# Copies by bank, one moved input sum and one moved product in a one-core hybrid decoder step

## The chip, the cores and the metric

The kernel runs on one core of a Trainium2 chip. The metric is the device time of one execution in microseconds (us), as the median over several runs; less is better. A core has TensorE for matrix products, VectorE and ScalarE for element-wise work on SBUF and PSUM, GpSimd for element-wise work on SBUF, and queues on which SyncE, ScalarE and GpSimd issue DMA transfers. Products are written to PSUM, which has eight banks.

## What the reference computes

One step of a decoder layer for 1024 prompt tokens and 64 sample tokens (8 sequences of 8 tokens), with a width of 1024. After a root-mean-square norm, one input projection feeds three branches: retention, multi-scale causal pooling, and sparse attention with a compressed, a selected and a window part. Each branch has a gate and a projection of its own; they are merged by sigmoid gates, projected once more, added to the input and normed. Cut to what the change touches:

```python
z = rms_norm(x, gain) @ w_in
(rq, rk, rv, rg, pu, pg, nq, ck, cv, sk, sv, wk, wv, nbg, ng, mg) = jnp.split(z, split_at, axis=-1)
blk = kv_cmp.reshape(n, nc, L_CMP, 2, NSA_KV_HEADS, dh) + pe_cmp   # compressed blocks of 32 tokens
cm = jnp.mean(blk, axis=2)
kc = jnp.einsum('ncgd,de->ncge', cm[:, :, 0], w_ck)
vc = jnp.einsum('ncgd,de->ncge', cm[:, :, 1], w_cv)
...
b_c = (jax.nn.silu(ng) * o_c) @ w_br_c
merged = gates[:, :, 0] * b_a + gates[:, :, 1] * b_b + gates[:, :, 2] * b_c
y = x + merged @ w_out
y_prompt = rms_norm(hp, final_gain)
```

## The kernel before

Every fp32 matrix is kept as two fp16 parts, high and low, so that one product is three fp16 products on TensorE (high by high, high by low, low by high). A weight is loaded in fp32 as `raw` and split by `wsplit`: ScalarE writes the high part, VectorE the low part. Two `raw` buffers take turns in the projection stage; four of the first eight loads go to parts of the query weights' tiles instead.

The tokens are nine tiles of 128 (the last holds the 64 sample tokens). `phase_kv` is the projection stage: `norm_first` norms the first tile, and TensorE writes it transposed into two PSUM banks, from which ScalarE copies the high part (L379) and VectorE subtracts to get the low part (L380), piece by piece. `kv_tile` projects keys and values, `q_tile` the queries, `cmp_means` the means of blocks of 32 tokens, `cmp_weights` loads the weights of the compressed branch (seven loads on SyncE and two small products, L490). After the last tile `cmp_prompt` makes the compressed keys (`kc`) and values (`vc`) for two groups: two products, then copies on ScalarE (L562, L568) and subtractions on VectorE (L563, L569).

`input_sums` makes eight units of sums and differences of quarters of the normed input for a later stage that multiplies by Strassen's scheme. A unit is four additions (L1221) and four subtractions (L1223) on VectorE, a copy to fp16 on ScalarE (L1224), a subtraction on VectorE (L1225) and a store to DRAM on SyncE's queue (L1226). The units are made between the tiles, one or two at a time, the last at n = 8.

The attention stage follows. `silu_c` first makes the sparse branch's gate (four weight columns of three segments; a segment is 24 products and a step on ScalarE and VectorE; a `yield` follows each eighth of it), then the heads' scores, probabilities and values are made, with the retention branch's gate and other gate products as filling. Scores are written to four rotating buffers with the tag "S"; probabilities are transposed by DMA into `pt`. Retention, pooling, sample attention and the merge stage come next.

`out_rows` is the output stage. It makes the last projection for 512 rows of either half by Strassen's scheme, as seven products per tile of 128 rows, 12 matmuls of 512 columns each (L1841). In a first round over four tiles it forms "11 by 11" and "12 by 21", which need no weight difference. `remainder` does the 64 rows that are left (L1881). A second round over the four tiles forms the other five. The four differences T1 to T4 of the output weights are made at the stage's start by VectorE (L1800) and split (L222, L223). `plus` adds a product to a row tile on VectorE (L1846).

The order in which each engine runs its instructions is fixed before the run by a planner that simulates the program with modelled times and gives priority to what is written first. `with self.behind()` puts each instruction of a block behind the last marked instruction on its own engine; `self.tc.issue_after(x)` does so only for the engine of x. Instructions that touch one PSUM bank on different engines are ordered one after the other.

Of the kernel before, what the change touches and what calls it, by code (L numbers as in the profile page):

```python
# [127 lines left out]
class Kern:  # L128
# [32 lines left out]
    def run(self):  # L161
        ctx = self.ctx
        right = ExitStack()
        self.setup(ctx)
        with ExitStack() as es:
            self.kvstore(es)
            with ExitStack() as e1:
                self.phase_kv(e1)
            rp = self.pool(right, "gate", side="right")
            self.ga = rp.tile([P, 8, NG, 2, 32], F16, tag="ga", name="ga", bufs=1)  # L170
            self.rp = rp
            self.gc = rp.tile([P, 4, NG, 2, 32], F16, tag="gc", name="gc", bufs=1)
            with ExitStack() as e1:
                sp = self.pool(e1, "attw", bufs=2)

                tp = self.pool(e1, "atth")
                ps = self.pool(e1, "aps", bufs=1, space=PSUM)
                self.pjb = A_PJ
                self.wq = self.nc.scalar
                self.eq = self.nc.scalar  # L180
                self.egd = self.dr.tile([8, P, NTOK], F32, name="egd")
                self.cgd = self.dr.tile([8, P, NTOK], F32, name="cgd")
                with self.behind():
                    deque(self.silu_c(tp, self.gc, C_NG, ps, self.wng), 0)
                fill = chain(self.silu_c(tp, self.ga, C_RG, ps), self.early_gates(tp, ps, range(N_FILL)))
                self.prompt_attention(sp, ps, fill)
                with self.tc.issue_after(self.after.ins):
                    deque(fill, 0)
                self.eq = self.nc.sync
        with ExitStack() as eo:  # L190
            self.smc = self.pool(eo, "smc")
            self.pjb = R_PJ
            with ExitStack() as es:
                self.psb, ppj, psa = [self.pool(es, x, bufs=1, space=PSUM) for x in ("rpsb", "rppj", "rpsa")]
                self.retention(es, ppj, psa, right)
            self.gbp = self.pool(right, "gbp", side="right")
            self.gb = self.gbp.tile([P, 4, NG, 2, 32], F16, tag="gb", name="gb", bufs=1)
            with ExitStack() as es:
                psb, ps, pst = [self.pool(es, x, bufs=1, space=PSUM) for x in ("spsb", "sppj", "spst")]
                sp = self.pool(es, "smp", bufs=1)  # L200
                pool = self.pooling(es, ps, pst)
                next(pool)
                with self.behind():
                    self.sample_attention(sp, psb, pst)
                next(pool, None)
                self.out_weights(self.pool(es, "wout"))
        with ExitStack() as es:
            self.output(es)
        right.close()
        if self.post:  # L210
            self.post(self)
# [143 lines left out]
    def norm_first(self, xp, ps):  # L355

        nc, d = self.nc, self.d
        x = self.load_x(xp, 0)
        nc.sync.dma_start(self.ident, d["c_ident"])
        gcol = xp.tile([P, 8], F32, name="gcol", bufs=1)  # L360
        nc.sync.dma_start(gcol, d["gain_cols"])
        xs = xp.tile([P, 1024], F32, tag="xs", name=self.nm("xs"), bufs=2)
        ss = xp.tile([P, 2], F32, tag="ss", name=self.nm("ss"), bufs=2)
        nc.scalar.activation(xs[:, :512], x[:, :512], AF.Square, accum_out=ss[:, 0:1])
        nc.vector.tensor_tensor_reduce(out=xs[:, 512:], in0=x[:, 512:], in1=x[:, 512:], scale=1.0, scalar=0.0,
                                       op0=ALU.mult, op1=ALU.add, accum_out=ss[:, 1:2])
        nc.vector.tensor_tensor(ss[:, 0:1], ss[:, 0:1], ss[:, 1:2], op=ALU.add)
        self.rsqrt(ss[:, 1:2], ss[:, 0:1], 1.0 / 1024)
        dg = xp.tile([P, P], F32, name="dg", bufs=1)
        nc.vector.tensor_scalar(dg, self.ident, ss[:, 1:2], None, op0=ALU.mult)  # L370
        self.first = []
        for q in range(2):
            tp = ps.tile([P, 4, P], F32, tag="tk", name=self.nm("tp"), bufs=2)
            for k in range(4):
                kk = q * 4 + k
                nc.tensor.matmul(tp[:, k, :], x[:, kk * P:(kk + 1) * P], dg, start=True, stop=True)
            for k in range(4):
                kk = q * 4 + k
                self.marks["ACT"] = nc.scalar.activation(self.xh[:, kk, :P], tp[:, k], AF.Copy, scale=gcol[:, kk:kk + 1])  # L379
                self.marks["DVE"] = nc.vector.scalar_tensor_tensor(  # L380
                    self.xl[:, kk, :P], tp[:, k], gcol[:, kk:kk + 1], self.xh[:, kk, :P],
                    op0=ALU.mult, op1=ALU.subtract)
            self.first.append(dict(self.marks))
# [117 lines left out]
    def phase_kv(self, es):  # L501
# [22 lines left out]
        for n in range(NT + 1):  # L524
            if n == 0:
                qh, ql = self.load_t(wk, [(C_NQ, 512)], "nq", 1, out=nq)
            if n + 2 < NT:
                self.norm_tile(kp, ps, gain, TILES[n + 2])
            if n == 0:
                self.cmp_weights(bp, ps)  # L530
            if n < NT:
                kvz = self.kv_tile(kp, bp, ps, kh, kl, TILES[n])
            if n:
                self.q_tile(kp, ps, qh, ql, TILES[n - 1])
            if n == NT:
                self.cmp_prompt(kp, ps, cmt)
            if n < NT and TILES[n] < 8:
                with self.tc.issue_after(self.marks["PE"].ins):
                    self.cmp_means(ps, kvz, cmt, TILES[n])
            if n == 3:  # L540
                self.bias_tables(bp, ps)

            if n == 4:
                sums = self.input_sums(kp)
            with self.behind():
                for _ in range((0, 0, 0, 0, 1, 2, 2, 2, 1, 0)[n]):
                    next(sums)
            if n == 7:
                with self.behind():
                    self.wng = self.load_c(d["w_in"][0][:, C_NG:C_NG + P])  # L550

    def cmp_prompt(self, kp, ps, cmt):
        nc = self.nc

        nc.vector.memset(self.vbd, 0.0)
        cmr = kp.tile([P, 4, 32], F32, name="cmr", bufs=1)
        nc.vector.tensor_copy(cmr, cmt[:, 1:2, :].to_broadcast([P, 4, 32]))
        for g in range(2):
            gr = slice(g * 64, g * 64 + 64)
            kc = ps.tile([P, 32], F32, tag="kc", name=self.nm("kc"), bufs=2)  # L560
            nc.tensor.matmul(kc, self.wckd[gr].rearrange("p a c -> p (a c)"), cmt[gr, 0, :], start=True, stop=True)
            nc.scalar.copy(self.kcst[:, g, 0, :], kc)  # L562
            nc.vector.tensor_tensor(self.kcst[:, g, 1, :], kc, self.kcst[:, g, 0, :], op=ALU.subtract)  # L563
            vc = ps.tile([P, 64], F32, tag="kc", name=self.nm("vc"), bufs=2)
            nc.tensor.matmul(vc, cmr[gr].rearrange("p a c -> p (a c)"), self.wcvd[gr], start=True, stop=True)
            for r in range(4):
                rr = slice(r * 32, r * 32 + 32)
                nc.scalar.copy(self.vbd[rr, g, 0, r, :], vc[rr])  # L568
                nc.vector.tensor_tensor(self.vbd[rr, g, 1, r, :], vc[rr], self.vbd[rr, g, 0, r, :], op=ALU.subtract)  # L569

    def kv_tile(self, kp, bp, ps, kh, kl, t):
# [635 lines left out]
                self.eq.dma_start(self.egd[e, :, s0:s0 + n], th[:, :n])  # L1207
                yield

    def input_sums(self, rp):  # L1210


        nc = self.nc
        self.txd = self.dr.tile([P, 4, 2, 4, 544], F16, name="txd")
        for c0 in (0, 272):
            for k in range(4):
                f = rp.tile([P, 4, 272], F32, tag="rsf", name=self.nm("rsf"), bufs=1)
                o = rp.tile([P, 4, 2, 272], F16, tag="rso", name=self.nm("rso"))
                for i, (kk, t) in enumerate(((k, 0), (k, 1), (k + 4, 1), (k + 4, 0))):
                    c = slice(t * 544 + c0, t * 544 + c0 + 272)  # L1220
                    nc.vector.tensor_tensor(f[:, i], self.xh[:, kk, c], self.xl[:, kk, c], op=ALU.add)  # L1221
# [1 line left out]
                    nc.vector.tensor_tensor(f[:, a], f[:, x], f[:, y], op=ALU.subtract)  # L1223
                nc.scalar.copy(o[:, :, 0], f)  # L1224
                nc.vector.tensor_tensor(o[:, :, 1], f, o[:, :, 0], op=ALU.subtract)  # L1225
                nc.sync.dma_start(self.txd[:, :, :, k, c0:c0 + 272], o)  # L1226
                yield

    def ga_at(self, j):
# [549 lines left out]
    def out_rows(self, ps, wk, mm, sx, wo, tb):  # L1779
# [116 lines left out]
        for i, c in enumerate(order):  # L1896
# [5 lines left out]
            nc.scalar.activation(u, p, AF.Copy, scale=IWS)  # L1902
            plus(x[:, :512], p, x[:, :512])
            plus(x[:, :512], prod("12", "21", c), x[:, :512])
            base.append((x, st, u))
        remainder()
        for i, c in enumerate(order):
# [7 lines left out]
            nc.gpsimd.tensor_tensor(b0, b0, u2, op=ALU.add)  # L1915
            p5 = prod("S1", "T1", c)
            plus(b0, p5, b0)
            plus(b0, prod("S4", "22", c), b0)
            square(x0, y0, s0, 1, P, 512, 512)
            finish(((0, c, P),), x0, y0, s0, P, 2)  # L1920
            plus(u3, prod("S3", "T3", c), u2)
# [46 lines left out]
```

## Time and profile before

| | |
|---|---|
| median of 3 runs | 1310.8 us (1307.58 to 1311.88) |
| the profiled execution's own time | 1306.29 us |
| its span, first to last instruction | 1304.5 us |
| mean granted TensorE clock | 0.987 |

The profile is of a single execution. Its span is the time between its first and last instruction; 1.8 us of its own time lie outside. All times of rows are counted from the start of the span.

### The profile page before, as it was taken

How to read it: one execution, taken by the hardware profiler on the slowest of the kernel's cores; microseconds unless marked ns; L12 is line 12 of the kernel's file. 1: busy time of each engine (PE TensorE's matmuls, PEld its weight loads, DVE VectorE, ACT ScalarE, POOL GpSimd, SP SyncE). 2: the span in 40 equal slices, each digit the busy share in tenths (PEclk: the TensorE clock that was granted, in tenths of full speed). 3: DMA queues.
4: the chain of work that ended last, by engine and by line, in shares of the span. 5: the costliest groups of instructions: out<-in, count | busy, mean ns of one | idle time of the engine just before them, and what ended most of it. 6: DMA issues, size and time to landing. Idle time of an engine off the chain costs nothing. (4 is left out here: it accounts for less than half of the span.)

```text
span 1304.5 us, 27795 instructions
## 1 busy us (share of the span) xinstructions
PE 1251.3 (96%) x10520; PEld 850.6 (65%) x10520; DVE 912.2 (70%) x2288; ACT 631.3 (48%) x1474; POOL 525.2 (40%) x561
## 2 busy tenths in 40 slices
PE   7999899989999989999999999999999999999997
PEld 4555566767677764555655565657788888888643
DVE  6648635788777864766766668663698877578975
ACT  5633436667676763555554454433544333213331
POOL 1122013567676751445553550101743566323133
PEclk9999899999999999999999999998999999999998
DMA  7766623698899996243741278327542211543632
GB/s 251 182 133 149 149 66 86 99 147 146 164 173 205 192 207 174 58 124 104 173 139 35 85 202 264 77 76 255 180 130 58 58 49 55 175 145 114 227 96 97
DMA packets 324315, 179.24 MB, mean 137 GB/s; under 512 B 204433, under 2 KB 298609, under 8 KB 323764
## 3 DMA queue, kind: packets, MB, share of 16 engines
q1 hardware_dynamic: 283844, 137.83, 45.3%
q10 hardware_dynamic: 35600, 26.32, 6.8%
q0 software_dynamic: 4736, 13.31, 3.2%
q8 instruction: 82, 1.34, 0.4%
q14 instruction: 53, 0.43, 0.1%
HBM read 98.80 MB, written 33.25 MB: 101 GB/s over the span
## 5 line engine op out<-in xcount | busy, mean ns | idle before, releaser
L761 POOL TENSOR_TENSOR hl<-S,hl 128x640 f16<-128x640 f32 (+7 forms) x128 | 153.8, 1210 | 142.5 <-DVE hl L760 96.6
L309 PE MATMUL pj<-xh,whi 128*128 128x384 f16 (+1 forms) x480 | 153.0, 319 | 2.4 <-ACT ue L1423 2.1
L310 PE MATMUL pj<-xl,whi 128*128 128x384 f16 (+1 forms) x480 | 153.0, 319 | 0.0
L311 PE MATMUL pj<-xh,wlo 128*128 128x384 f16 (+1 forms) x480 | 152.8, 318 | 0.0
L288 PE MATMUL z<-rwh,xh 128*128 128x512 f16 x256 | 97.0, 379 | 0.0
L290 PE MATMUL z<-rwh,xl 128*128 128x512 f16 x256 | 97.0, 379 | 0.0
L289 PE MATMUL z<-rwl,xh 128*128 128x512 f16 x256 | 97.0, 379 | 0.0
L756 ACT ACTIVATE S<-S,nm 128x640 f32<-128x640 f32 (+7 forms) x128 | 93.7, 732 | 5.2 <-DVE hst L852 0.9
L311 PEld LDWEIGHTS <-wlo 128*128 128x128 f16 x672 | 66.1, 98 | 36.6 <-issue 1.3
L310 PEld LDWEIGHTS <-whi 128*128 128x128 f16 x672 | 66.1, 98 | 36.1 <-issue 4.9
L1572 DVE TENSOR_TENSOR q<-st,q 128x288 f32<-128x288 f32 (+1 forms) x168 | 70.3, 433 | 26.4 <-PE st L1563 25.3
L309 PEld LDWEIGHTS <-whi 128*128 128x128 f16 x672 | 66.1, 98 | 33.6 <-issue 1.3
L288 PEld LDWEIGHTS <-xh 128*128 128x128 f16 x448 | 45.3, 101 | 46.4 <-issue 7.2
L290 PEld LDWEIGHTS <-xl 128*128 128x128 f16 x448 | 43.9, 98 | 44.9 <-issue 0.7
L222 ACT ACTIVATE whi<-raw 128x1024 f16<-128x1024 f32 (+1 forms) x48 | 45.5, 948 | 57.0 <-PE pj L310 14.7
L289 PEld LDWEIGHTS <-xh 128*128 128x128 f16 x448 | 43.9, 98 | 42.1 <-issue 0.9
L755 ACT ACTIVATE hl<-S,nm 128x128 f16<-128x128 f32 (+7 forms) x64 | 49.1, 767 | 36.6 <-DMA pt<-hl 36.5
L1328 PE MATMUL o<-vst,pt 128*128 128x64 f16 x528 | 56.3, 193 | 10.7 <-DMA pt<-hl 10.6
L760 DVE CAST hl<-S 128x640 f16<-128x640 f32 (+4 forms) x64 | 33.2, 519 | 45.9 <-ACT S L756 16.2
L1260 POOL TENSOR_TENSOR rh<-rot,rh 128x256 f16<-128x256 f32 (+1 forms) x36 | 26.5, 735 | 89.1 <-ACT rh L1259 88.9
L310 PE MATMUL eg<-xl,whi 128*128 128x384 f16 (+1 forms) x192 | 61.5, 320 | 0.0
L309 PE MATMUL eg<-xh,whi 128*128 128x384 f16 (+1 forms) x192 | 61.5, 320 | 0.0
(511 smaller groups left out, 4056.0 us busy)
## 6 DMA issues: line engine op xcount, KB each, us to landing
raw<-w_in SPq DMA_DIRECT2D x26, 512.0 KB
raw<-w_in ACTq DMA_DIRECT2D x18, 512.0 KB
raw<-w_in SPq DMA_DIRECT2D x48, 128.0 KB
wad<-q ACTq DMA_DIRECT2D x21, 256.0 KB
txd<-rso SPq DMA_DIRECT2D x8, 544.0 KB
raw<-egd SPq DMA_DIRECT2D x16, 272.0 KB
s<-state_ret SPq DMA_DIRECT2D x16, 256.0 KB
o_ret_s<-s POOLq DMA_DIRECT2D x16, 256.0 KB
```

Source lines behind the costliest of these rows:

```text
L222: a = nc.scalar.activation(hi, raw, AF.Copy, scale=WS)
L288: nc.tensor.matmul(out, xh, hi[:, k, c0:c0 + n], start=(k == 0), stop=False)
L289: nc.tensor.matmul(out, xh, lo[:, k, c0:c0 + n], start=False, stop=False)
L290: self.marks["PE"] = nc.tensor.matmul(out, xl, hi[:, k, c0:c0 + n], start=False, stop=(k == 7))
L309: nc.tensor.matmul(out, hi[:, k, :], xh, start=(k == 0), stop=False)
L310: nc.tensor.matmul(out, hi[:, k, :], xl, start=False, stop=False)
L311: self.filled = nc.tensor.matmul(out, lo[:, k, :], xh, start=False, stop=(k == 7))
L755: nc.scalar.activation(hl[:, :w], s[:, d0:c1], AF.Exp, bias=nm[:, br:br + 1], scale=0.125)
L756: nc.scalar.activation(s[:, c0:c1], s[:, c0:c1], AF.Exp, bias=nm[:, br:br + 1], scale=0.125, accum_out=l[:, 0, br, r:r + 1])
L761: nc.gpsimd.tensor_tensor(hl[:, w:2 * w], s[:, d0:c1], hl[:, :w], op=ALU.subtract)
L1328: nc.tensor.matmul(out, lhs[0], rhs[0], start=start, stop=False)
L1572: nc.vector.tensor_tensor(out[:, c0:c0 + n], b, x[:, c0:c0 + n], op=ALU.add)
```

## The change

Five edits. In the first tile, the four copies of a bank are written before its four subtractions. The compressed branch's weights are asked for behind the first tile's projection, with their products behind its last one. In `cmp_prompt` a group's keys and values share one bank, each group has a bank of its own, both products come first, and all copies precede the subtractions. The last unit of the input sums is made behind the sparse branch's gate in program order, in two buffers of the scores' tag, and stored through GpSimd's queue; the first gate segment is placed behind TensorE's mark alone. In the output stage, the product S4 by 22 moves from the second round to the first.

```diff
@@ run
+                score = lambda: sp.tile([P, 1664], F32, tag="S", name=self.nm("sum"), bufs=LAG + 1)
+                self.sums_room = lambda: (score()[:, :1088].rearrange("p (i c) -> p i c", i=4),
+                                          score()[:, :1088].bitcast(F16).rearrange("p (i a c) -> p i a c", i=4, a=2))
+                self.sums_queue = self.nc.gpsimd
+                gates = self.silu_c(tp, self.gc, C_NG, ps, self.wng)
+                with self.tc.issue_after(self.marks["PE"].ins):
+                    for _ in range(8):
+                        next(gates)
                 with self.behind():
-                    deque(self.silu_c(tp, self.gc, C_NG, ps, self.wng), 0)
+                    deque(gates, 0)
+                    deque(self.sums, 0)
@@ norm_first
                 self.marks["ACT"] = nc.scalar.activation(self.xh[:, kk, :P], tp[:, k], AF.Copy, scale=gcol[:, kk:kk + 1])
+            for k in range(4):
+                kk = q * 4 + k
                 self.marks["DVE"] = nc.vector.scalar_tensor_tensor(
@@ phase_kv
-            if n == 0:
-                self.cmp_weights(bp, ps)
             if n < NT:
                 kvz = self.kv_tile(kp, bp, ps, kh, kl, TILES[n])
+            if n == 0:
+                with self.tc.issue_after(self.marks["PE"].ins):
+                    self.cmp_weights(bp, ps)
...
-                sums = self.input_sums(kp)
+                self.sums_room = lambda: (kp.tile([P, 4, 272], F32, tag="rsf", name=self.nm("rsf"), bufs=1),
+                                          kp.tile([P, 4, 2, 272], F16, tag="rso", name=self.nm("rso")))
+                self.sums_queue = nc.sync
+                sums = self.sums = self.input_sums()
             with self.behind():
-                for _ in range((0, 0, 0, 0, 1, 2, 2, 2, 1, 0)[n]):
+                for _ in range((0, 0, 0, 0, 1, 2, 2, 2, 0, 0)[n]):
@@ cmp_prompt
-        for g in range(2):
+        for g, tag in enumerate(("kc", "cm")):
             gr = slice(g * 64, g * 64 + 64)
-            kc = ps.tile([P, 32], F32, tag="kc", name=self.nm("kc"), bufs=2)
+            cc = ps.tile([P, 96], F32, tag=tag, name=self.nm("kc"), bufs=1)
+            kc, vc = cc[:, :32], cc[:, 32:]
             nc.tensor.matmul(kc, self.wckd[gr].rearrange("p a c -> p (a c)"), cmt[gr, 0, :], start=True, stop=True)
+            nc.tensor.matmul(vc, cmr[gr].rearrange("p a c -> p (a c)"), self.wcvd[gr], start=True, stop=True)
+            rows = [slice(r * 32, r * 32 + 32) for r in range(4)]
             nc.scalar.copy(self.kcst[:, g, 0, :], kc)
+            for r, rr in enumerate(rows):
+                nc.scalar.copy(self.vbd[rr, g, 0, r, :], vc[rr])
             nc.vector.tensor_tensor(self.kcst[:, g, 1, :], kc, self.kcst[:, g, 0, :], op=ALU.subtract)
-            vc = ps.tile([P, 64], F32, tag="kc", name=self.nm("vc"), bufs=2)
-            nc.tensor.matmul(vc, cmr[gr].rearrange("p a c -> p (a c)"), self.wcvd[gr], start=True, stop=True)
-            for r in range(4):
-                rr = slice(r * 32, r * 32 + 32)
-                nc.scalar.copy(self.vbd[rr, g, 0, r, :], vc[rr])
+            for r, rr in enumerate(rows):
                 nc.vector.tensor_tensor(self.vbd[rr, g, 1, r, :], vc[rr], self.vbd[rr, g, 0, r, :], op=ALU.subtract)
@@ input_sums
-                f = rp.tile([P, 4, 272], F32, tag="rsf", name=self.nm("rsf"), bufs=1)
-                o = rp.tile([P, 4, 2, 272], F16, tag="rso", name=self.nm("rso"))
+                f, o = self.sums_room()
...
-                nc.sync.dma_start(self.txd[:, :, :, k, c0:c0 + 272], o)
+                self.sums_queue.dma_start(self.txd[:, :, :, k, c0:c0 + 272], o)
@@ out_rows, first round
             plus(x[:, :512], prod("12", "21", c), x[:, :512])
+            plus(x[:, 512:], prod("S4", "22", c), x[:, 512:])
@@ out_rows, second round
             plus(b0, p5, b0)
-            plus(b0, prod("S4", "22", c), b0)
             square(x0, y0, s0, 1, P, 512, 512)
```

## Rows read from the trace of the kernel before

**Rows 1.** The page: busy us, share of the span and instructions by engine.

```profile
PE 1251.3 (96%) x10520; PEld 850.6 (65%) x10520; DVE 912.2 (70%) x2288; ACT 631.3 (48%) x1474; POOL 525.2 (40%) x561
```

**Rows 2.** Busy time by stretch; last: granted clock, DMA share, GB/s.

```profile
7.00:17.00 10.00, 6.89 (x34) 4.90 (x33) 5.73 (x12) 5.99 (x14) 0.39 (x1) 1.00 0.97 345
17.00:21.00 4.00, 4.00 (x17) 2.62 (x17) 3.89 (x5) 3.66 (x7) 0.16 (x1) 0.57 0.59 179
138.00:147.00 9.00, 5.06 (x36) 3.16 (x33) 7.95 (x20) 6.05 (x14) 0.00 (x0) 0.82 0.60 137
147.00:151.00 4.00, 4.00 (x15) 1.91 (x15) 0.65 (x3) 1.40 (x4) 0.00 (x0) 0.54 1.22 290
151.00:191.00 40.00, 39.70 (x295) 25.81 (x294) 15.93 (x51) 15.69 (x46) 4.21 (x10) 1.00 0.36 84
1212.50:1233.30 20.80, 20.80 (x99) 9.36 (x96) 20.80 (x33) 9.89 (x18) 3.53 (x3) 1.00 0.73 246
1238.70:1243.00 4.30, 2.08 (x12) 0.80 (x9) 4.04 (x7) 3.78 (x9) 0.00 (x0) 0.99 0.55 184
1243.00:1247.00 4.00, 4.00 (x12) 1.47 (x11) 4.00 (x9) 3.12 (x8) 0.00 (x0) 0.58 0.00 0
```

**Rows 3.** TensorE's waits over the span: us in total, times, longest.

```profile
PE o L1328 <- DMA pt<-hl: 10.6, 12, 3.9
```

**Rows 4.** First tile: its copies, subtractions and their waits, then TensorE by time.

```profile
L379 ACT ACTIVATE xh<-tp,gcol x8: 358/367/368, 8.6 to 14.2; 128x128 f16<-128x128 f32 x8
  DVE xl L380: 2.5, 5
...
L380 DVE SCALAR_TENSOR_TENSOR xl<-tp,gcol,xh x8: 342/350/353, 9.0 to 14.6; 128x128 f16<-128x128 f32 x8
  ACT xh L379: 2.8, 6
...
15.36 0.49 PE L288 MATMUL pj<-kvh,xh 128*128 128x512 f16 x2 [1.37 <-ACT kvh L222]
16.50 0.57 PE L490 MATMUL pmps<-a,pe 32*128 32x1 f32 x4 [0.65 <-DMA pe<-pe_cmp]
```

**Rows 5.** The last key weight's load and splits by time, and the next hole.

```profile
17.57 0.38 SPq L255 DMA_DIRECT2D raw<-w_in  x1
20.73 0.86 ACT L222 ACTIVATE kvh<-raw 128x792 f16<-128x792 f32 x1 [0.34 <-DMA raw<-w_in]
23.48 0.98 DVE L223 SCALAR_TENSOR_TENSOR kvl<-raw,kvh 128x792 f16<-128x792 f32 x1
36.29 0.61 PE L612 MATMUL tk<-id,kd 128*128 128x128 f16 x8 [1.52 <-DVE xl L410]
```

**Rows 6.** Between projection and branch gates, by time.

```profile
140.13 1.50 DVE L1221 TENSOR_TENSOR rsf<-xh,xl 128x272 f32<-128x272 f16 x4
143.77 0.61 PE L695 MATMUL tq<-id,qs 64*64 64x64 f16 x8 [1.98 <-DVE qs L682]
146.50 0.69 PE L565 MATMUL vc<-wcvd,cmr 64*128 64x64 f32 x2 [1.56 <-DVE kcst L563]
```

**Rows 7.** The sums' lines: duration ns min/median/max, first and last start.

```profile
L1223 DVE TENSOR_TENSOR rsf<-rsf x32: 370/441/443, 84.8 to 145.5; 128x272 f32<-128x272 f32 x32
L1224 ACT CAST rso<-rsf x8: 1090/1096/1098, 86.9 to 150.2; 128x1088 f16<-128x1088 f32 x8
L1225 DVE TENSOR_TENSOR rso<-rsf,rso x8: 1291/1292/1539, 88.0 to 151.3; 128x1088 f16<-128x1088 f32 x8
```

**Rows 8.** Output stage by time, TensorE and VectorE.

```profile
1225.88 1.27 DVE L1846 SCALAR_TENSOR_TENSOR xr<-py,xr 128x512 f32<-128x512 f32 x2
1233.38 5.42 PE L1881 MATMUL py<-wo,mm 128*32 128x256 f16 x192
1242.81 0.93 PE L1841 MATMUL py<-tb,T 128*128 128x512 f16 x2 [1.91 <-DVE tb L223]
1247.67 0.69 DVE L223 SCALAR_TENSOR_TENSOR T4a<-q,T4a 128x512 f16<-128x512 f32 x1
```

More of the change, by code (lines that the diff above doesn't have):

```diff
@@ L1208, in early_gates, with input_sums @@
                 yield
-    def input_sums(self, rp):
+    def input_sums(self):
         nc = self.nc
```

## The prediction, made before the change was run

> **What bounds the kernel now.** I read the page first: TensorE is busy for 96% of the span, VectorE for 70% and no other engine for more than 48% [rows 1]. So time can only be won where TensorE stands still or runs at its lower clock, and the second view, the busy time by stretch, was used to find those places near the edits. There are three [rows 2]. In 7 to 17 us, where the first token tile is projected, TensorE is busy 6.89 of 10 us, and the next 4 us run at a granted clock of 0.57, that is mostly at 1.2 GHz. In 138 to 147 us, between the projection stage and the branch gates, it is busy 5.06 of 9 us, and the 4 us behind are granted 0.54. In 1238.7 to 1243 us, at the start of the output stage's second round, it is busy 2.08 of 4.30 us, and the 4 us behind are granted 0.58. The third view, TensorE's waits over the whole span, shows that the largest single cause lies elsewhere: 10.6 us in 12 holes for transposed probabilities [rows 3]. No edit is aimed at that. The last view, the order of instructions, tells which wait ends last in each of the three holes.
>
> What a hole costs is its idle time and the slow clock behind it. The slow part is worth, from the granted clock, (1 - 0.57) x 4 = 1.7 us at the start, (1 - 0.54) x 4 = 1.8 us at the stage change and (1 - 0.58) x 4 = 1.7 us in the output stage. The three ceilings are thus 3.11 + 1.7 = 4.8, 3.94 + 1.8 = 5.7 and 2.22 + 1.7 = 3.9 us, 14.4 us together.
>
> **Edit 1, the first tile's copies, and edit 2, the compressed keys' weights behind the tile.** Eight ScalarE copies of 0.37 us and eight VectorE subtractions of 0.35 us empty two banks. They alternate, copy and subtraction of one piece, and VectorE stood 2.8 us before six of its eight for a copy, ScalarE 2.5 us before five of its own [rows 4]. Nothing is added or removed; with four copies and then four subtractions a bank is handed over once, not seven times. I count one hand-over of the six waits per bank as left, 2 x 2.8/6 = 0.9 us, so VectorE's stream is 1.9 us shorter. The price is that the first subtraction comes three copies later, 3 x 0.37 = 1.1 us; TensorE has the copies' own products to do meanwhile, and if they don't cover it, it comes off the 1.9 us. TensorE pays through the weight splits behind: it waited 1.37 us for the third piece's split [rows 4], and the last piece's VectorE split runs from 23.48 to 24.46 us [rows 5]. That last piece also has a bound that the edit doesn't touch: its load was issued at 17.57 us, behind the small loads on SyncE's queue, and ScalarE waited for it until 20.73 us [rows 5]. With 0.86 us of ScalarE and 0.98 us of VectorE behind that, the split can't end before 22.6 us, 1.9 us earlier than now. The two answers agree at 1.9 us.
>
> Edit 2 moves two small products, which made TensorE wait 0.65 us for their load [rows 4], behind the tile. Its seven loads keep their place among SyncE's loads, since the tile between issues none there; VectorE's copy of their result moves back too, and only the tile's own means, later on TensorE, wait for it. I put it at 0.1 us, the rest being inside the wait for the third split. Together 2.0 us. Below: nothing, if the next hole, 1.52 us at 36.29 us for the third tile's normalisation [rows 5], just grows by as much. Above: 4.8 us. I keep 2.0 because that hole hangs on VectorE and on the loads that wait for the same splits, and both move up with them.
>
> **Edit 3, a bank for each group of compressed keys.** Four bank uses become two, in separate banks. The second group's value product waited 1.56 us for the first group's subtractions [rows 6]; that wait has no cause left, and I take all of it. Instructions, their number and their shapes stay.
>
> The Trainium skill (PSUM — Partial Sum Buffer, section on bank collisions) speaks against this edit: it says that two engines must not be in one bank and 32-partition quadrant at once, two readers included. By it a group's five subtractions now start behind its five copies. No row of the kernel before has keys and values in one bank; by the nearest rows, 0.37 us a copy, this delays them by at most 1.9 us. The sum by the rule is the same unless TensorE waits for that bank, and then 1.9 us less.
>
> **Edit 4, one input sum moved behind the stage change.** Eight units of sums are made; the last leaves. It is four additions of 1.50 us together [rows 6], four subtractions of 0.44, a copy of 1.10 on ScalarE, a subtraction of 1.29 and one store [rows 7], so 4.6 us of VectorE. Its additions stand directly in front of the subtraction on which TensorE's sample queries waited 1.98 us [rows 6]; I take 1.5 us of that wait. The unit then runs beside the branch gates, where VectorE is busy 15.93 of 40 us and ScalarE 15.69 [rows 2]: 4.6 and 1.1 us fit in, cost nothing. If they did not, each microsecond by which a gate's own VectorE step is late would stop TensorE once its two product banks are full. The store goes from SyncE's queue to GpSimd's, where it waits for the unit's last subtraction with the heads' remainders queued behind it; in 151 to 191 us GpSimd is busy 4.21 us [rows 2], and its result is read only in the merge stage, hundreds of microseconds later. Letting the first gate unit and the second gate weight load go without the other engines' marks can fill what is left of the hole; I count nothing for it.
>
> The stage change gives 1.56 + 1.5 = 3.1 us. Below: 1.5 us, if the gates' banks come free only with the sample queries' copies. Above: 5.7 us, if the gate unit fills the hole and the clock stays up.
>
> **Edit 5, S4's product in the first round.** Nothing is removed: four products of 20.80/8 = 2.6 us [rows 2] change place. The second round began when the first round and the 5.42 us remainder were done, and its first product waited for the weight differences, 1.91 of the hole's 2.22 us at once for VectorE's part of one [rows 8]. Now 10.4 us of work that needs none of them stands in front. VectorE is full there, 20.80 of 20.80 us [rows 2], and gets four additions, 4 x 0.64 = 2.5 us [rows 8], so the differences come 2.5 us later and are wanted 10.4 us later: 7.9 us of margin for a 2.2 us hole. What they hang on, the loads of the output weights, isn't moved. Four more banks are in use at once, of eight, while VectorE lags; its last difference ended at 1248.36 us [rows 8], still before the new end of the first round and the remainder plus 1.9 us. The hole goes and with it the slow clock: 3.9 us. Below: 2.2 us, if the clock falls anyway. The last iteration loses a product, but its end hangs on S3's product, which keeps its place from the end: nothing.
>
> **The sum.** 2.0 + 3.1 + 3.9 = 9.0 us. Against the profiled execution's own 1306.3 us that makes 1297.3. That execution is 4.5 us below the median of the three runs, 1310.8, and below all three; taken from the median, the forecast is **1301.8 us**.
>
> At the start and the stage change I count no clock, because those holes shrink and do not close. The Trainium skill (TensorE: Matmul & The Clock Gate, What's actually happening) says that the throttled state is the default and that activity lifts it. By that rule alone, all three slow stretches would go wherever TensorE is kept busy, 12.5 us and 1298.3; the rows agree that each slow stretch lies behind a hole, and show none at these places without one.
>
> **Rivals.**
> *Only the output stage pays.* The start stays tied to the load issued at 17.57 us and the third tile's hole takes up what is won; at the stage change the gates wait for banks. For it speaks that both are chains of several engines; against it, that VectorE's waits stand in both. Gain 3.9 us: 1306.9 us.
> *Slower, through the score buffers.* The moved unit holds two of the four score buffers of the attention stage, and the third and fourth head must wait for it and its store. If it runs late, heads start late, the gate products that fill TensorE's holes are used up first, and the waits for transposed probabilities, 0.88 us a hole [rows 3], multiply. It decides from 9.0 us on, about ten more holes; with fifteen, 13.2 us, the time is 1310.8 + 4.2 = 1315 us. For it: these waits exist. Against it: the unit has all of the 40 us in which VectorE is 40% busy.
> *The change doesn't do what it says.* Each engine's order is laid by a planner from modelled times, so a hole that is closed in one place can open again at the next wait of the same chain. Then the time stays within the spread of the runs, 1307.6 to 1311.9.
>
> **Chances and range.** About 0.3% (3.9 us) is what a measurement of this kernel can tell from no change. The forecast holds with 0.60: its own range is 1296.4 (all ceilings) to 1305.4 us (0 + 1.5 + 3.9 = 5.4 us gained, the lower bounds of the two early places). Only the output stage: 0.17, half of it beyond 0.3%. Score buffers: 0.10, slower. No effect: 0.13, of which 0.03 slower. So faster 0.69, same 0.18, slower 0.13. For the range I go from the ceilings, less the runs' spread of 3.2 us, 1293, up to 1312, which leaves out the slower rival.
>
> **What would show it.** Right: in the first tile, four copies in a row with no wait between them, and the last split ending near 22.6 us; between the stages, both groups' products together and the value product's wait gone, the sample queries' wait near 0.5 us; in the output stage, no wait for a weight difference at the start of the second round and a granted clock of 1.00 behind it. Wrong: the third tile's hole at about 3.5 us, a hole before the first gate product as long as now, or more than 12 holes for transposed probabilities.

## The result, and the profile after

The changed kernel is faster by about 0.6%: 1300.9 us median of 4 runs (1299.5 to 1306.3) against 1311.0 us of 4 runs of the kernel before beside it, ratio 0.9937, 95% interval 0.9911 to 0.9963. The forecast was 1301.8 us. A second, longer measurement (below, *again*) gave 0.9952, 0.9935 to 0.9969. The sum thus came out, but not by its terms: the output stage gave nothing that can be measured, and the gain comes from the two early places.

The two profiled executions hide the gain: both spans are 1304.5 us. The one of the changed kernel was its slowest run (1306.3 us), the one of the kernel before lay below all of its timed runs. So no gain is read from these two spans; places are compared, and later several profiles.

Busy time by stretch of the changed kernel, as in [rows 2]:

```profile
7.00:17.00 10.00, 9.36 (x46) 6.37 (x47) 7.64 (x15) 7.22 (x16) 0.55 (x1) 1.00 0.98 344
17.00:21.00 4.00, 4.00 (x27) 2.35 (x25) 3.47 (x6) 3.62 (x6) 0.38 (x1) 1.00 0.58 185
138.00:147.00 9.00, 8.33 (x64) 5.00 (x62) 7.64 (x26) 5.32 (x16) 0.00 (x0) 1.00 0.39 89
147.00:151.00 4.00, 4.00 (x29) 2.52 (x28) 3.29 (x6) 1.69 (x3) 0.00 (x0) 1.00 0.98 250
1240.00:1250.00 10.00, 10.00 (x214) 6.94 (x213) 9.91 (x18) 4.98 (x10) 0.00 (x0) 1.00 0.22 78
```

All three holes are shut or nearly so: TensorE is busy 9.36 of 10, 8.33 of 9 and 10 of 10 us (8.58 to 9.01 of the first 10 us in the seven other profiles with edits 1 and 2, below), and the granted clock behind each is 1.00, where it was 0.57, 0.54 and 0.58. Next the start by time; the brackets hold the engine's idle time before the row and what ended it, and line numbers stand 10 to 21 higher than before:

```profile
8.86 1.14 ACT L389 ACTIVATE xh<-tp,gcol 128x128 f16<-128x128 f32 x4 [1.82 <-PE tp L386]
10.03 1.13 DVE L392 SCALAR_TENSOR_TENSOR xl<-tp,gcol,xh 128x128 f16<-128x128 f32 x4 [1.98 <-ACT xh L389]
...
16.07 0.53 SPq L265 DMA_DIRECT2D raw<-w_in  x1
...
22.41 0.23 DVE L480 CAST wmask<-wm 128x128 bf16<-128x128 f32 x1 [1.94 <-DMA wm<-c_wmask]
22.55 0.98 DVE L233 SCALAR_TENSOR_TENSOR kvl<-raw,kvh 128x792 f16<-128x792 f32 x1
...
24.36 1.06 ACT L404 ACTIVATE xs<-x 128x1024 f32<-128x1024 f32 x1 [3.54 <-DMA x<-x_prompt]
...
30.34 0.28 PE L298 MATMUL pj<-kvh,xh 128*128 128x280 f16 x1 [2.15 <-ACT kvz L327]
```

The copies come four in a row and the bank is handed over once [rows 4]. The last weight's split ends at 23.5 us, 0.9 us earlier than in [rows 5], not 1.9, since a mask that VectorE waits for stands in front of it. Its load was issued at 16.07 us, 1.5 us earlier than in [rows 5]: the bound that the forecast took as untouched moved too. The third tile's hole at 36.29 us is gone, but a new one of 2.15 us stands at 30.34 us: ScalarE, which empties the banks in its own order, had stood 3.54 us for a token tile's load.

The stage change, beside [rows 6]:

```profile
141.50 1.05 ACT L714 COPY qsts<-tq 128x512 f16<-128x512 f16 x2
...
142.52 0.85 ACT L583 CAST vbd<-kc 32x64 f16<-32x64 f32 x4
142.60 0.32 PE L319 MATMUL pj<-xh,whi 128*128 128x384 f16 x1 [0.67 <-ACT qsts L714]
...
143.40 0.19 DVE L584 TENSOR_TENSOR kcst<-kc,kcst 128x32 f16<-128x32 f32 x1 [0.82 <-ACT vbd L583]
```

Both waits of [rows 6] are gone; 0.67 us is left in front of the first gate product. VectorE's subtractions of a group do start behind that group's last copy, for which VectorE stood 0.82 us, and TensorE doesn't wait for them.

The end of the output stage, which the forecast costed at nothing. `py<-T4a,mm` are a tile's last products, `u<-py,raw` makes u3, the sum of S3's product and an earlier sum of the tile, and L1878 scales the two halves of a finished tile, 512 columns each, for their store:

```profile
1279.92 0.68 DVE L1862 SCALAR_TENSOR_TENSOR u<-py,raw 128x512 f32<-128x512 f32 x1
1280.67 2.43 DVE L1878 SCALAR_TENSOR_TENSOR rm<-xr,yst,rm 128x512 f32<-128x512 f32 x2
...
1285.80 2.78 PE L1857 MATMUL py<-T4a,mm 128*128 128x320 f16 x24
...
1287.13 2.49 DVE L1878 SCALAR_TENSOR_TENSOR rm<-rm,yst 128x512 f32<-128x512 f32 x2
1287.15 1.27 POOL L1932 TENSOR_TENSOR xr<-xr,raw 128x512 f32<-128x512 f32 x1
...
1289.55 0.68 DVE L1862 SCALAR_TENSOR_TENSOR xr<-py,xr 128x512 f32<-128x512 f32 x1
...
1292.42 1.42 DVE L1878 SCALAR_TENSOR_TENSOR rm<-xr,yst,rm 128x512 f32<-128x512 f32 x2 [0.73 <-POOL yst L429]
...
1293.76 0.68 DVE L1862 SCALAR_TENSOR_TENSOR u<-py,raw 128x512 f32<-128x512 f32 x1
1294.57 1.26 POOL L1938 TENSOR_TENSOR rm<-rm,u 128x512 f32<-128x512 f32 x1 [2.18 <-issue]
...
1300.44 0.37 ACTq L1880 DMA_DIRECT2D o_y_p<-rm  x1
```

TensorE starts its last products at 1285.80 us, so S3's product of the last tile is done by then. VectorE turns it into u3 at 1293.76 us, 8 us later: in its order the scaling of the tile's first half (1292.42 us) comes first, and that waits for an addition, ScalarE's squares and GpSimd's root. In the third tile, the first two rows, u3 comes ahead of that scaling. The last tile in the kernel before:

```profile
1292.19 2.78 PE L1841 MATMUL py<-T4a,mm 128*128 128x320 f16 x24
...
1293.68 0.68 DVE L1846 SCALAR_TENSOR_TENSOR u<-py,raw 128x512 f32<-128x512 f32 x1
```

TensorE ends 6.4 us earlier and the kernel ends at the same time.

### The profile page after: what moved, and what is told of

It reads as the page before. It is cut to its first block, busy times and chain, and to the rows that moved or that the text cites. A ratio compares the mean times of both kernels' runs of the same rounds, so it can differ in the third digit from the quotient of the medians.

```text
span 1304.5 us, 27790 instructions
## 1 busy us (share of the span) xinstructions
PE 1251.2 (96%) x10520; PEld 849.4 (65%) x10520; DVE 912.6 (70%) x2288; ACT 630.8 (48%) x1474; POOL 524.8 (40%) x562
## 5 line engine op out<-in xcount | busy, mean ns | idle before, releaser
L1344 PE MATMUL o<-vst,pt 128*128 128x64 f16 x528 | 56.7, 194 | 11.6 <-DMA pt<-hl 11.3
L321 PE MATMUL eg<-xh,wlo 128*128 128x384 f16 (+1 forms) x192 | 62.1, 323 | 0.0
```

Of the source, the lines that this page charges most:

```text
L321: self.filled = nc.tensor.matmul(out, lo[:, k, :], xh, start=False, stop=(k == 7))
L1344: nc.tensor.matmul(out, lhs[0], rhs[0], start=start, stop=False)
```

## The experiments

All ratios are to the kernel before, run beside each of them.

**again**: the changed kernel once more.

> The changed kernel once more, for a tighter ratio and a second profile. Both theories expect a ratio near the 0.9937 seen. The first profile of the changed kernel lasted 1306.3 us, its slowest run, and showed TensorE's last product ending 6.4 us earlier than before (1288.3 against 1294.7 us) with the end of the span unmoved at 1304.5 us. Theory A, edit 5's gain is real: in a profile of a typical run the span ends about 9 us earlier and the stretch from TensorE's last product to the end is nearer the 9.8 us of before than the 16.2 us seen. Theory B, VectorE's fixed order in the output stage is late whatever TensorE does: the stretch is again near 16 us.

Ratio 0.9952 (0.9935 to 0.9969), 1303.2 us against 1308.8. In its profile TensorE's last product ends 15.6 us before the end of the span, in the first 15.9, in the kernel before 9.5, as theory B says.

**only_out**: the kernel before with edit 5 alone.

```diff
             plus(x[:, :512], prod("12", "21", c), x[:, :512])
+            plus(x[:, 512:], prod("S4", "22", c), x[:, 512:])
...
             plus(b0, p5, b0)
-            plus(b0, prod("S4", "22", c), b0)
```

> The kernel before with edit 5 alone. Theory A (the prediction's step): 3.9 us, ratio 0.9970, with the hole of 2.22 us before the second round gone. Theory B: the hole is gone at TensorE, whose last product ends about 4 us earlier against the first output product, but VectorE, which follows a fixed order and waits in it for ScalarE and GpSimd, ends where it ended: ratio 0.9990 to 1.0005.

Ratio 1.0013 (0.9994 to 1.0032). The last T4 products, u3 and the last store by time:

```profile
1291.78 2.78 PE L1841 MATMUL py<-T4a,mm 128*128 128x320 f16 x24
...
1299.23 0.68 DVE L1846 SCALAR_TENSOR_TENSOR u<-py,raw 128x512 f32<-128x512 f32 x1
...
1305.92 0.37 ACTq L1864 DMA_DIRECT2D o_y_p<-rm  x1
```

u3 starts 7.5 us behind the T4 products again. Edit 5 alone gives nothing that can be measured; A's 0.9970 lies outside the interval, so B.

**no_out**: the changed kernel with edit 5 taken back (the diff above, reversed).

> The changed kernel without edit 5 (S4 by 22 back in the second round). Theory A: 2.0 + 3.1 = 5.1 us of the gain stay, ratio 0.9961. Theory B: nearly the whole gain comes from the start and the stage change, 8 us or more, ratio 0.9940 or less.

Ratio 0.9948 (0.9931 to 0.9966), as good as with edit 5. It lies between the two theories, and its interval holds both A's 0.9961 and B's 0.9940. The same three rows:

```profile
1287.61 2.78 PE L1857 MATMUL py<-T4a,mm 128*128 128x320 f16 x24
...
1289.11 0.69 DVE L1862 SCALAR_TENSOR_TENSOR u<-py,raw 128x512 f32<-128x512 f32 x1
...
1295.80 0.37 ACTq L1880 DMA_DIRECT2D o_y_p<-rm  x1
```

u3 starts 1.5 us behind the T4 products, as before the change. By this ratio and that of *only_out*, the whole gain comes from edits 1 to 4.

**tail1, tail1_b**: the changed kernel with u3 ahead of the first half's scaling, measured twice.

```diff
-            nc.vector.scalar_tensor_tensor(out, py, IWS, x, op0=ALU.mult, op1=ALU.add)
+            return nc.vector.scalar_tensor_tensor(out, py, IWS, x, op0=ALU.mult, op1=ALU.add)
...
             square(x0, y0, s0, 1, P, 512, 512)
-            finish(((0, c, P),), x0, y0, s0, P, 2)
-            plus(u3, prod("S3", "T3", c), u2)
+            u3i = plus(u3, prod("S3", "T3", c), u2)
             nc.gpsimd.tensor_tensor(b1, b1, u3, op=ALU.add)
+            with self.tc.issue_after(u3i.ins):
+                finish(((0, c, P),), x0, y0, s0, P, 2)
             plus(b1, p5, b1)
```

> The changed kernel with one more change of order in the output stage's second round: S3's product and its addition (u3) are placed ahead of the scaling and storing of the tile's first half, so that GpSimd's two additions of u3 and what hangs on them start earlier. Theory B (the tail hangs on VectorE's order: in the changed kernel's profile u3 of the last tile was made at 1293.76 us though its product was complete about 8 us earlier): the end comes 3 to 6 us earlier than in the changed kernel, ratio to the kernel before 0.989 to 0.992. Theory A (the tail hangs on TensorE's last product): no difference to the changed kernel, 0.9937.

> The changed kernel with u3 ahead of the scaling of the first half, a second time, as the base for the two variants beside it. Theory B: ratio 0.990 to 0.994 again, and 9.5 us from TensorE's last product to the end, where the changed kernel has 15.6 to 15.9 us. Theory A: near the changed kernel's 0.995.

Ratios 0.9925 (0.9896 to 0.9954) and 0.9919 (0.9895 to 0.9943), the fastest of all with the variant below. By time, in *tail1_b*:

```profile
1287.36 2.78 PE L1857 MATMUL py<-T4a,mm 128*128 128x320 f16 x24
1287.56 0.69 DVE L1862 SCALAR_TENSOR_TENSOR u<-py,raw 128x512 f32<-128x512 f32 x1 [0.50 <-PE py L1857]
...
1292.17 1.41 DVE L1878 SCALAR_TENSOR_TENSOR rm<-xr,yst,rm 128x512 f32<-128x512 f32 x2
```

Now u3 waits for TensorE (0.50 us) and no longer for its turn on VectorE, and the scaling falls behind it. From TensorE's last product to the end it is 9.5 and 9.6 us again. The order on VectorE was the cause. In time, *tail1* is 4.6 us below *again* by the medians of one series, though the intervals of the two ratios overlap.

**only_start**: the kernel before with edits 1 and 2 (the `norm_first` hunk of the change and the first part of its `phase_kv` hunk); **only_copies**: with edit 1, the `norm_first` hunk, alone.

> The kernel before with edits 1 and 2 alone. Theory A (the prediction's sum): 2.0 us, ratio 0.9985, with the hole in 7 to 17 us reduced by about 2 us. Theory C (the start's gain is spent again before the stage change): the hole in 7 to 17 us is nearly gone and the clock behind it stays up, as in the changed kernel, but new waits for ScalarE, which stands in order behind the loads of the next tiles, take it back: in the two profiles so far the keys' products of the stage change begin at 140.3 us with and without it. Ratio 0.9995 to 1.0005.

> The kernel before with edit 1 alone, four copies of a bank ahead of its four subtractions. Theory A: 1.9 of the 2.0 us of the start come from it, ratio 0.9985, and the last key weight's split ends near 22.6 us. Theory C: the copies' order closes most of the hole in 7 to 17 us by itself, and the gain is spent before 140 us: ratio 0.9995 to 1.0005.

Ratios 0.9977 (0.9956 to 0.9998) and 0.9994 (0.9974 to 1.0013). For both together A was nearer, though the interval reaches into C's. Alone, edit 1 gives nothing that can be measured, nearer to C, with A's 0.9985 inside the interval; its profile keeps a wait of 0.77 us for the load that edit 2 moves, and has new ones, 2.8 us for ScalarE's bank copy and 2.0 us for a query weight's split. What theory C says of the later loads is there too, in part: a hole of 1.6 to 2.3 us near 30 us stands in all eight profiles with edits 1 and 2, and in five of them the clock falls behind it, as in *again*:

```profile
30.25 0.28 PE L298 MATMUL pj<-kvh,xh 128*128 128x280 f16 x1 [2.24 <-ACT kvz L327]
```

```profile
30.00:32.00 2.00, 1.75 (x12) 1.32 (x12) 1.99 (x5) 2.00 (x7) 1.29 (x2) 0.81 0.88 278
32.00:34.00 2.00, 2.00 (x11) 1.40 (x10) 2.00 (x7) 2.00 (x6) 0.00 (x0) 0.50 1.66 208
```

The second fence is the busy time by stretch: granted 0.50, that is 1.2 GHz, in 32 to 34 us, though TensorE is busy throughout. Another hole, of 0.9 to 2.1 us near 70 us, again for ScalarE's bank copy (`kvz`), stands in six of the eight, but not in *only_start* and *tail1*; in four of the six the clock falls behind it too (0.57 in 72 to 76 us of *again*).

**only_stage**: the kernel before with edits 3 and 4; **only_banks**: edit 3 alone; **only_sum**: edit 4 alone.

> The kernel before with edits 3 and 4 alone. Theory A: 3.1 us, ratio 0.9976. Theory C (the stage change carries nearly all of the gain, since the hole closes and the slow clock behind it goes): the ceiling of 5.7 us or more, ratio 0.9957 or less; the first score product begins about 6 us after where it now stands less, near 150.5 us.

> The kernel before with edit 3 alone, a bank for each group of compressed keys. Theory A: the value product's wait of 1.56 us goes and nothing takes its place: ratio 0.9988. Rival: the products behind it wait for VectorE anyway (sample queries, 1.98 us), whose four additions of an input sum stand ahead of them: ratio 1.000, and only edit 4 together with edit 3 closes the hole.

> The kernel before with edit 4 alone (the last input sum moved, the first gate segment placed behind TensorE's mark only). In profiles, edits 3 and 4 together bring the first score product from 16.4 to 10.0 us behind the first product of compressed keys, edit 3 alone lengthens it to 19.4 us. Theory A (terms add): 1.5 us of the sample queries' wait go, the value product's 1.56 us stay: the distance is about 14 us. Theory E (edit 4 closes the hole, and the banks add little): about 11 us, ratio like that of both together, 0.9997 within its interval of 0.0021.

Ratios 0.9997 (0.9976 to 1.0019), 1.0043 (1.0024 to 1.0062) and 0.9995 (0.9976 to 1.0014). With both, the first score product comes at 152.6 us, 4 us earlier than before (156.7) and 2 us later than C said, and 10.0 us behind the first compressed-key product instead of 16.4. The time shows nothing of it: C's 0.9957 is outside the interval, A's 0.9976 at its edge. In this profile, some 12 us later, part of it is lost again, by time and by stretch:

```profile
165.04 0.24 PE L1341 MATMUL o<-vst,pt 128*128 128x64 f16 x1 [3.17 <-DMA pt<-hl]
```

```profile
163.00:167.00 4.00, 1.96 (x8) 0.99 (x9) 0.55 (x1) 1.86 (x8) 0.43 (x1) 0.62 0.21 40
167.00:171.00 4.00, 4.00 (x14) 1.91 (x13) 0.77 (x4) 0.88 (x4) 0.85 (x2) 0.53 0.00 0
```

The first head's value product waits 3.17 us for its transposed probabilities, and the clock falls behind it. The slow clock costs (1 - 0.50) x 1.96 = 1.0 us in the first row, where TensorE is busy only from 165.04 us on, granted 0.50, and (1 - 0.53) x 4 = 1.9 us in the second, 2.9 us more. The same hole is 2.00 us in *only_sum* and 2.25 in *tail1*, with the slow clock behind, 1.0 us or less in the other five with the unit beside the gates (none in *again* and *no_early*), and missing in the six without. With edit 4 alone the distance is 13.0 us, between A's 14 and E's 11, and the first score product comes 1.5 us earlier than before.

Edit 3 alone makes the kernel slower, which neither theory said. Its profile, of the fastest of its twelve runs, has the first score product 4.1 us later than before (160.8 us). By time:

```profile
149.08 0.60 ACT L674 ACTIVATE qs<-pj 128x512 f16<-128x512 f32 x1 [3.84 <-DMA qst<-qs]
...
150.51 1.06 ACT L698 COPY qsts<-tq 128x512 f16<-128x512 f16 x2
...
151.62 0.48 PE L309 MATMUL pj<-xh,whi 128*128 128x384 f16 x1 [6.12 <-ACT qsts L698]
```

The value product's wait is gone, and TensorE waits 6.12 us in front of the first gate product instead: on ScalarE the sample queries' copy came to stand behind the compressed keys' copies and an activation that waits 3.84 us for the transposition of the queries before it. In the changed kernel that copy stands ahead of the keys' copies (141.50 us in the fence above).

**no_early**: as *tail1_b*, the first gate segment placed behind all engines' marks again.

```diff
                 gates = self.silu_c(tp, self.gc, C_NG, ps, self.wng)
-                with self.tc.issue_after(self.marks["PE"].ins):
-                    for _ in range(8):
-                        next(gates)
```

> As tail1_b, with the first gate segment again placed behind all engines' marks, as in the kernel before. Theory A (the prediction counted nothing for this placement): no difference to tail1_b, the hole before the first gate product as short as there (0.7 us). Rival: the early gate products are what fills the hole; without them the first score product comes 2 to 4 us later behind the first product of compressed keys, and the slow clock behind the hole returns.

Ratio 0.9967 (0.9947 to 0.9986): 5.1 us slower than *tail1_b* by the medians. The wait and the clock behind it:

```profile
141.16 0.48 PE L316 MATMUL pj<-xh,whi 128*128 128x384 f16 x1 [2.86 <-ACT qsts L711]
```

```profile
140.00:144.00 4.00, 2.84 (x10) 1.28 (x10) 2.74 (x8) 1.11 (x3) 0.00 (x0) 0.54 1.23 259
144.00:147.00 3.00, 3.00 (x11) 1.44 (x10) 0.00 (x0) 0.00 (x0) 0.00 (x0) 0.50 1.35 189
```

The hole and the slow clock are back, and the first score product comes 15.8 us behind the first compressed-key product, not 10.1. That is the rival's reading, and more than its 2 to 4 us. The profiles' ends differ by 2.3 us only, and the first score products by 0.6 us, since TensorE came to the stage change 5.1 us earlier in *no_early*. Among other things its hole near 70 us was 0.9 us with no slow clock behind, where *tail1_b* had 2.1 us with one, and it has no hole near 124 us. That last one, 1.1 to 1.3 us for VectorE's part of the last tile's keys (`kd`), stands in all eight profiles with edit 4 and its early gate segment and in none of the other six, so it is a price of that edit.

**late_sum**: as *tail1_b*, the moved unit behind the whole attention.

```diff
                 with self.behind():
                     deque(gates, 0)
-                    deque(self.sums, 0)
...
                     deque(fill, 0)
+                with self.tc.issue_after(self.filled.ins):
+                    deque(self.sums, 0)
```

> As tail1_b, with the moved unit of the input sums put behind the whole attention instead of beside the branch gates, so that it holds no score buffer while heads are computed. Theory D (the prediction's rival of the score buffers, in small): with the unit beside the gates TensorE waited 11.3 to 13.8 us for transposed probabilities in five profiles, without it 9.2 to 10.8 us in five; the wait returns to about 10 us and the kernel is some 2 us faster than tail1_b, ratio lower by 0.0015. Rival: the longer waits come from the attention starting 6 us earlier against the same loads, whatever the unit holds: the wait stays at 12 us, and no difference.

Ratio 0.9921 (0.9897 to 0.9945), no difference to *tail1_b*. TensorE's waits for transposed probabilities, first *tail1_b*, then *late_sum*:

```profile
PE o L1344 <- DMA pt<-hl: 12.0, 12, 4.0
```

```profile
PE o L1345 <- DMA pt<-hl: 9.6, 11, 2.5
```

The wait falls as theory D says; its rival, that the wait hangs on the attention's earlier start, is out, since the first score stands at 150.8 us here and 151.3 in *tail1_b*. In eight profiles with the unit beside the gates it is 11.3 to 13.8 us, mean 12.0; in six without, this one among them, 9.2 to 10.8, mean 10.0. The times can't show it: each of the two ratios is uncertain by 0.0024, 3.1 us, more than the 2.4 us at stake.

## Why the prediction was right in its sum, and where not

The landmarks are starts and ends of products in single profiles, in us. The first is the first score product of the attention, the last two are the output stage from its first product to TensorE's last, and from there to the end.

| kernel | edits | first score | output: TensorE | then to the end |
|---|---|---|---|---|
| before | none | 156.7 | 82.4 | 9.5 |
| only_out | 5 | 157.0 | 78.2 | 15.4 |
| only_copies | 1 | 161.2 | 82.5 | 9.6 |
| only_start | 1, 2 | 154.5 | 80.8 | 9.5 |
| only_banks | 3 | 160.8 | 80.8 | 9.5 |
| only_sum | 4 | 155.2 | 82.4 | 9.6 |
| only_stage | 3, 4 | 152.6 | 82.4 | 9.6 |
| no_out | 1 to 4 | 152.4 | 80.9 | 9.5 |
| after | all | 150.4 | 78.3 | 15.9 |
| again | all | 151.9 | 78.2 | 15.6 |
| tail1 | all, u3 first | 148.3 | 78.2 | 9.5 |
| tail1_b | all, u3 first | 151.3 | 78.2 | 9.6 |
| no_early | as tail1_b, no early segment | 151.9 | 78.2 | 10.3 |
| late_sum | as tail1_b, unit last | 150.8 | 78.2 | 10.1 |

**Edit 5, the step that failed.** "The last iteration loses a product, but its end hangs on S3's product, which keeps its place from the end: nothing." S3's product keeps its place, but the end hangs on u3, and u3 on VectorE's order. S4's product had been the cover for the chain in front of it: with it TensorE takes 13.0 us a tile, and VectorE keeps abreast, u3 0.2 us behind the T4 products in the first tile and 1.4 to 1.5 in the others (*before* and *no_out*). Without it TensorE takes 10.4 us. VectorE then comes 6.3 to 7.0 us late into the round (why was not tried apart), catches up to 4.1 to 4.5 us by the third tile, where u3 stands ahead of the scaling, and falls back to 7.5 to 8.0 us in the last, where the scaling stands first and u3 comes 13.7 to 13.9 us behind the one before. TensorE's part was forecast well: 82.4 to 78.2 us, 4.2, where the slow clock had been, as in four of seven profiles without edit 5, and 80.8 to 78.2, 2.6, where not; 3.9 and 2.2 were said. The term that was missing is the 6.0 us (9.5 to about 15.6) given back behind TensorE. By the profiles the output stage is 1.6 to 3.9 us longer with edit 5, 93.6 to 94.2 against 90.3 to 92.0 us; by the times, 1.0013 and the pair 0.9952 and 0.9948, it is worth nothing. With u3 moved, it is 87.7 to 88.5 us in four profiles.

**Edits 1 and 2.** Right in size: 2.0 us forecast; with them the first score comes 2.4 us earlier without edits 3 and 4 (156.9, the mean of two profiles, to 154.5) and 1.7 us with them (152.6 to 150.9, the mean of five); timed, 0.9977, 3.0 us. The way was another. The hole shut almost wholly and the slow clock behind it went, which was the ceiling of 4.8, and new holes near 30 and 70 us, most often with the slow clock behind them, took some of that back. Whether edit 2, put at 0.1 us, is worth more stays open: edit 1 alone gives nothing that can be measured, but the two intervals overlap, and edit 2 was not run alone.

**Edits 3 and 4.** 3.1 us forecast; at the first score 4.3 us (156.9 to 152.6) or 3.6 (154.5 to 150.9). The two waits of the forecast went, and the slow clock too, which it had not counted; the hole near 124 us is already taken off these numbers. Two terms were wrong. "That wait has no cause left, and I take all of it": alone, edit 3 goes with an order in which a copy that TensorE needs stands behind a transfer, and costs 5.6 us. "I count nothing for it", of the first gate segment: without it the hole and its clock are back. What closes the hole is that the sample queries' copy comes early on ScalarE. Edit 4 with its early segment brings it ahead of most of the keys' copies, both edits together ahead of all, and without the early segment it stands behind them.

**The score buffers.** The rival's wait exists and is small: 2.0 us more in the mean (12.0 against 10.0) for transposed probabilities, in 10 to 15 holes where there were 10 to 12, not the 9 us from which it would have decided. More than half of it, 1.2 us in the mean of the eight, falls on the first head, which the unit delays; that the buffers do it and not VectorE's time for the unit was not tried apart.

**The sum.** 6.0 us at the first score, less 2.0 in the attention, plus nothing from the output stage make 4.0. Measured are 8.3 us by the first ratio and 6.3 by the second (*again*, 4.1 to 8.5), and 6.8 us for edits 1 to 4 alone, 4.4 to 9.0. So the 9.0 us forecast were rather too many, edits 1 to 4 made up for a part of edit 5's missing 3.9 us (6.8 where 5.1 were said, within the interval), and the median of 1300.9 us came as near to 1301.8 as it did partly by the spread of four runs. From 2.3 to 4.3 us lie between what the landmarks show and what the times show. They stay open: runs of one kernel differ by 5 us and more, the slow stretches behind small holes fall in other places in each profile, and from the first score to the output stage's first product, where the edits change only the moved unit, the profiles take anything from 1055.9 to 1063.4 us. Open too is whether the parts simply add: edits 1 and 2 and edits 3 and 4 measured singly make 0.9974, together 0.9948, and the intervals allow the one as well as the other.

**The clock.** The rule of the Trainium skill (TensorE: Matmul & The Clock Gate, What's actually happening) would have all three slow stretches go once TensorE is kept busy. At the three places the trace agrees, 1.00 in each; the 12.5 us that it would make did not come, since edit 5's share was given back behind TensorE and the holes that appeared elsewhere have slow stretches of their own.

## What to carry to other kernels

A product that is moved off the end of an engine's work takes its cover with it: before counting the hole that it fills elsewhere, read how far each in-order engine behind it lags, and whether it can follow if TensorE comes sooner. Where it cannot, the remedy is to reorder the lagging engine, here one step put ahead of another, worth some 4 us by the times and 6 us by the profiles. And an edit that removes a wait can be worth nothing or less alone, because a planned order moves other work with it; read the order of the engine that ends the next wait before adding terms.

## What the runs showed of the hardware

VectorE's pair of 128x512 scalings (L1878) took 1.42 us with GpSimd idle (1292.42 us in the changed kernel) and 2.49 us when a GpSimd addition of 1.27 us began 0.02 us later (1287.13 us); both rows stand above. In *only_out* both engines lost:

```profile
1286.28 2.44 DVE L1862 SCALAR_TENSOR_TENSOR rm<-xr,yst,rm 128x512 f32<-128x512 f32 x2
1286.35 1.82 POOL L1922 TENSOR_TENSOR rm<-rm,u 128x512 f32<-128x512 f32 x1
```

The pair took 2.44 us and GpSimd's addition 1.82 us where 1.26 us is its time alone (1300.05 us there). The Trainium skill (SBUF — State Buffer, SBUF: two separate sides) says that a VectorE operation with two SBUF inputs and a GpSimd operation that reads SBUF take turns on a shared port pair, whole instruction by whole instruction. These rows agree: the 1.0 to 1.1 us lost is somewhat less than one addition. It adds to the lag of VectorE in the output stage.
